# Channel shuffle on one core: giving even and odd tiles each their own DMA queue

## The chip, the cores and the metric

The kernel runs on one core of one Trainium2 chip. A core has five engines that run side by side and are kept in step by semaphores, and a set of 16 DMA engines that move data between device memory and the on-chip buffer of 128 partitions (SBUF). A transfer is started by an instruction that sits in the instruction queue of one of the engines; here SyncE (SP in the profile) and ScalarE (ACT) do that, and neither computes anything. VectorE (DVE) does the only computation. The metric is device time in microseconds of one execution.

## The reference

The input is a float32 array of 16 x 64 x 64 pixels with 256 channels. The channels are seen as 8 groups of 32 and the two axes are swapped, so nothing is calculated: 67.11 MB are read, their order within each pixel is changed, and 67.11 MB are written.

```python
batch, h, w, c = x.shape            # 16, 64, 64, 256
x = x.reshape(batch, h, w, groups, c // groups)     # groups = 8
x = x.transpose(0, 1, 2, 4, 3)
x = x.reshape(batch, h, w, c)
```

## The kernel before

The pixels are cut into 16 tiles. A tile of size q holds 128 x q pixels, q of them in each partition, so every partition's share of a tile is one contiguous run of q x 1024 bytes in memory. The sizes (`_SIZES`) grow at the start and shrink at the end: 4, 8, 16, then twelve times 38, then 28. In bytes: 512 KB, 1 MB, 2 MB, twelve times 4864 KB, 3584 KB.

Each tile t goes through three steps, called here Lt, Ct and St:

- **Lt**, the load into an input buffer (line 47), issued from SyncE's queue.
- **Ct**, one VectorE copy from the input buffer to an output buffer that swaps the two channel axes by its access patterns (line 49).
- **St**, the store of the output buffer (line 53), issued from ScalarE's queue.

There are three input buffers (`_IN_BUFS`) and two output buffers (`_OUT_BUFS`). So L(t+3) may start only when Ct has read its buffer, and C(t+2) may start only when St has landed. The order of the instructions in each queue is the order of the program text (`manual_schedule`), and the waits on semaphores are put in by the framework. SyncE's queue therefore holds L0, L1, L2, ... and ScalarE's holds S0, S1, S2, ...; each engine sends its instructions in that order, and one that waits holds up those behind it. The transfers that a queue has sent form one line of rows on each of the 16 DMA engines; a row is what one partition gets or gives, 38912 bytes for the tiles of size 38. A transfer of 128 rows gives 8 rows to each DMA engine, and a closing packet of a few bytes that reports completion.

Of the kernel before, what the change touches and what calls it, by code (L numbers as in the profile page):

```python
# [1 line left out]

# [4 lines left out]


F32 = mybir.dt.float32
P = 128  # L10

_SIZES = [4, 8, 16] + [38] * 12 + [28]
_IN_BUFS = 3
_OUT_BUFS = 2


@with_exitstack
def kernel(
    ctx: ExitStack,
    tc: tile.TileContext,  # L20
    x: bass.AP,
    groups: bass.AP,
    out: bass.AP,
):
    nc = tc.nc
    b, h, w, c = x.shape
    G = int(groups)
    CPG = c // G
    assert G * CPG == c
    assert sum(_SIZES) * P == b * h * w  # L30
    biggest = max(_SIZES)

    x_flat = x.rearrange("b h w c -> (b h w c)")
    out_flat = out.rearrange("b h w c -> (b h w c)")

    in_pool = ctx.enter_context(tc.tile_pool(name="in_pool", bufs=_IN_BUFS))
    out_pool = ctx.enter_context(tc.tile_pool(name="out_pool", bufs=_OUT_BUFS))

    def rows(flat, first, q):

        return flat[first * c : (first + P * q) * c].rearrange("(p f) -> p f", p=P)

    ctx.enter_context(tc.manual_schedule(engines=None))
    first = 0
    for q in _SIZES:
        in_tile = in_pool.tile([P, biggest * c], F32, name="in_tile")
        nc.sync.dma_start(out=in_tile[:, : q * c], in_=rows(x_flat, first, q))  # L47
        out_tile = out_pool.tile([P, biggest * c], F32, name="out_tile")
        nc.vector.tensor_copy(  # L49
            out=out_tile[:, : q * c].rearrange("p (i j g) -> p i j g", j=CPG, g=G),  # L50
            in_=in_tile[:, : q * c].rearrange("p (i g j) -> p i j g", g=G, j=CPG),
        )
        nc.scalar.dma_start(out=rows(out_flat, first, q), in_=out_tile[:, : q * c])
        first += P * q


# [1 line left out]
_INS = ['x', 'groups']  # L58
_OUTS = [((16, 64, 64, 256), 'float32')]

_NUMBERS = {'groups': 8}


# [26 lines left out]
```

## Time and profile before

| | |
|---|---|
| median of 3 runs | 316.71 us (316.44 to 317.62) |
| the profiled execution's own time | 316.46 us |
| its span (first to last instruction) | 314.7 us |
| VectorE busy | 119.2 us, 16 copies |
| one copy of size 38 | 8802 ns mean |
| DMA traffic | 134.22 MB, mean 427 GB/s over the span |

The profile was taken on one execution. Its span leaves 1.76 us of that execution's own time outside (316.46 less 314.7). "Time to landing" is the time from the start of the issuing instruction to the moment at which all 16 DMA engines have reported completion. q1 is the DMA queue fed by SyncE and q10 the one fed by ScalarE. A view over a short window counts a packet in the window in which it starts.

### The profile page before, as it was taken

Reading aid. Unit: us, or ns where it says so; the run is one execution under the profiler, and the core shown is the slowest. Engines: PE = TensorE matmul, PEld = TensorE weight load, DVE = VectorE, ACT = ScalarE, POOL = GpSimd, SP = SyncE. Lnnn points to the kernel's source line nnn. Section 1 sums busy time; section 2 is a strip of 40 time slices with the busy share of each in tenths; the row PEclk is TensorE's granted clock in tenths of the full one; section 3 lists DMA queues with packets and bytes.
Section 4 is the critical chain, followed back from the end, with each engine's and each line's share of the span. In section 5 each row is a group of like instructions: output and inputs, shape, how many; then the busy total and the mean of one; then the engine's idle time right before and its main releaser. Section 6 shows DMA issues by size and latency. Waiting matters only on the chain.

```text
span 314.7 us, 133 instructions
## 1 busy us (share of the span) xinstructions
DVE 119.2 (38%) x16; POOL 0.2 (0%) x4
## 2 busy tenths in 40 slices
DVE  3040645505506407407308209109109019046620
POOL 0000000000000000000000000000000000000000
DMA  8999999999999999999999999999999999999997
GB/s 308 452 398 454 413 419 466 396 475 396 455 415 445 425 430 440 425 445 415 455 396 470 401 465 406 460 411 460 411 460 411 460 411 455 428 395 454 455 418 306
DMA packets 4608, 134.22 MB, mean 427 GB/s; under 512 B 512, under 2 KB 512, under 8 KB 768
## 3 DMA queue, kind: packets, MB, share of 16 engines
q1 hardware_dynamic: 2304, 67.11, 49.8%
q10 hardware_dynamic: 2304, 67.11, 49.4%
HBM read 67.11 MB, written 67.11 MB: 427 GB/s over the span
## 4 chain that ended last, share of the span: by engine, by line
DMA 75%; DVE 20%; issue 0%; SPq 0%; DVEq 0%
DMA out_dram<-out_tile 74%; DVE out_tile L49 20%; DMA in_tile<-in_x_dram 2%; SPq L47 0%; DVEq L49 0%
## 5 line engine op out<-in xcount | busy, mean ns | idle before, releaser
L49 DVE COPY out_tile<-in_tile 128x9728 f32<-128x9728 f32 (+4 forms) x16 | 119.2, 7449 | 181.4 <-DMA out_dram<-out_tile 175.9
L71 POOL MEMSET const-bfloat16-1.0<- 128x1 bf16 x1 | 0.1, 102 | 0.0
L71 POOL MEMSET const-uint8-127<- 128x1 uint8 x1 | 0.1, 102 | 0.0
L71 POOL MEMSET const-float32-1.0<- 128x1 f32 x1 | 0.1, 99 | 0.0
L71 POOL MEMSET const-float32-0.0<- 128x1 f32 x1 | 0.1, 98 | 0.2 <-issue 0.2
## 6 DMA issues: line engine op xcount, KB each, us to landing
in_tile<-in_x_dram SPq DMA_DIRECT2D x12, 4864.0 KB, 46.8
out_dram<-out_tile ACTq DMA_DIRECT2D x12, 4864.0 KB, 37.0
in_tile<-in_x_dram SPq DMA_DIRECT2D x1, 3584.0 KB, 43.8
out_dram<-out_tile ACTq DMA_DIRECT2D x1, 3584.0 KB, 13.3
in_tile<-in_x_dram SPq DMA_DIRECT2D x1, 2048.0 KB, 11.0
out_dram<-out_tile ACTq DMA_DIRECT2D x1, 2048.0 KB, 26.7
in_tile<-in_x_dram SPq DMA_DIRECT2D x1, 1024.0 KB, 5.4
out_dram<-out_tile ACTq DMA_DIRECT2D x1, 1024.0 KB, 25.8
```

The source lines that it names most:

```text
L49: nc.vector.tensor_copy(out=out_tile[:, : q * c].rearrange("p (i j g) -> p i j g", j=CPG, g=G), in_=in_tile[:, : q * c].rearrange("p (i g ...
L71: nc = _bacc.Bacc("TRN2", target_bir_lowering=False, num_devices=1)
```

## The change

Before, all loads are issued by SyncE and all stores by ScalarE. After, tile t's load and its store are both issued by the same engine: SyncE for even t, ScalarE for odd t. The loads are also written out in another place of the program: the first three stand ahead of the loop, and L(t+3) is issued in iteration t, after St. Sizes, buffers, the copy and all transfers stay as they are.

```diff
-    first = 0
-    for q in _SIZES:
-        in_tile = in_pool.tile([P, biggest * c], F32, name="in_tile")
-        nc.sync.dma_start(out=in_tile[:, : q * c], in_=rows(x_flat, first, q))
+    firsts = [P * sum(_SIZES[:t]) for t in range(len(_SIZES))]
+    in_tiles = {}
+
+    def queue(t):
+
+        return nc.scalar if t % 2 else nc.sync
+
+    def load(t):
+        q = _SIZES[t]
+        in_tiles[t] = in_pool.tile([P, biggest * c], F32, name="in_tile")
+        queue(t).dma_start(
+            out=in_tiles[t][:, : q * c], in_=rows(x_flat, firsts[t], q)
+        )
+
+    for t in range(_IN_BUFS):
+        load(t)
+    for t, q in enumerate(_SIZES):
+        in_tile = in_tiles.pop(t)
         out_tile = out_pool.tile([P, biggest * c], F32, name="out_tile")
         nc.vector.tensor_copy(
...
-        nc.scalar.dma_start(out=rows(out_flat, first, q), in_=out_tile[:, : q * c])
-        first += P * q
+        queue(t).dma_start(
+            out=rows(out_flat, firsts[t], q), in_=out_tile[:, : q * c]
+        )
+        if t + _IN_BUFS < len(_SIZES):
+            load(t + _IN_BUFS)
```

The two queues then hold:

```
SyncE   : L0 L2 S0 L4 S2 L6 S4 L8 ... L14 S12 S14
ScalarE : L1 L3 S1 L5 S3 L7 S5 L9 ... L15 S13 S15
```

## The prediction

> **What bounds the kernel now.** I read the page's slices first. The DMA row stands at 9 in nearly every slice, while the DVE row swings between 0 and 9, so the 16 DMA engines are the resource that is never free.
>
> ```profile
> DVE  3040645505506407407308209109109019046620
> DMA  8999999999999999999999999999999999999997
> ```
>
> Next comes the chain that ended last. It is store, copy, store, copy to the end: each copy waits for the store two tiles back to give its output buffer free. The groups say the same in time: almost all of VectorE's idle time ends with a store.
>
> ```profile
> DMA out_dram<-out_tile 74%; DVE out_tile L49 20%; DMA in_tile<-in_x_dram 2%; SPq L47 0%; DVEq L49 0%
> L49 DVE COPY out_tile<-in_tile 128x9728 f32<-128x9728 f32 (+4 forms) x16 | 119.2, 7449 | 181.4 <-DMA out_dram<-out_tile 175.9
> ```
>
> That chain could be read as "the buffers bound it". The third view corrects this: the DMA view over two steady tile periods, 74 to 120 us, then over the end, 290 to 313 us.
>
> ```profile
> DMA packets 576, 19.92 MB, mean 433 GB/s; under 512 B 64, under 2 KB 64, under 8 KB 64
> q1 hardware_dynamic: 288, 9.96, 50.1%
> q10 hardware_dynamic: 288, 9.96, 50.1%
> ```
>
> ```profile
> DMA packets 325, 9.90 MB, mean 430 GB/s; under 512 B 37, under 2 KB 37, under 8 KB 37
> q10 hardware_dynamic: 325, 9.90, 99.6%
> ```
>
> Two things are to be seen. With both queues at work each gets half of the packets and of the time, and the sum is 433 GB/s; with one queue alone, stores only, it is 430 GB/s. So the rate depends neither on how many queues are filled nor on the mix of reads and writes. And the engines are full: the stores are slow because they share, not because they start late.
>
> A row's price follows. In the timeline the copies of size 38 start 22.97 us apart in the middle (143.32, 166.32, 189.28, 212.26). In such a period a DMA engine moves 8 rows of a load and 8 of a store, so a 38912-byte row takes 22.97 / 16 = 1.436 us. All rows: 16 x 1.436 x (12 + 56/38) = 309.6 us, where 56 is 4 + 8 + 16 + 28. The span is 314.7: some 1.7 us pass before the first row moves, 0.8 lie behind the last landing (the last store is issued at 300.6 and lands after 13.3), and 2.6 are lost in and around the small rows of the start. No order of transfers can gain more than these few; the order can lose, wherever both queues are empty at once.
>
> **What the Trainium skill says.** "DMA: Bandwidth & Descriptors", section "Issuing engines are not separate DMA queues": transfers from sync and scalar run on the same 16 engines and interleave, and issuing from several saves only issue time. The 433 and 430 GB/s above agree. The same page, "Queues, rings and completion order": a DMA engine takes turns between the queues packet by packet, and within a queue takes them in ring order. The 288 against 288 packets agree. "Perfetto Trace Analysis", "DMA Optimizations", advises one engine for inputs and another for outputs, to allow more dynamic spread; that is the arrangement of before, and no trace here prices leaving it.
>
> **The change part by part.** *Issue time.* The tile view has 16 load issues of 328 ns on SP and 16 store issues of 362 ns on ACT. After, each engine issues 8 and 8; nothing else runs on either, so nothing is delayed by more than one issue, 0.36 us, and that lies under rows already in line. Cost 0 in the middle; without the cover, 0.4 us.
>
> *Waits in a queue.* SyncE has L4 (waits for C1), S2 (C2), L6 (C3), S4 (C4); ScalarE has S1 (C1), L5 (C2), S3 (C3). Both are in the order of the copies, so no instruction holds up one that is ready. When Ct ends, St and L(t+3) are both free and stand at the heads of different queues, as before. Cost 0.
>
> *The lines on the DMA engines.* This is the real change. St no longer has a line of stores before it but L(t+2), and L(t+3) stands behind S(t-1). Suppose L(t+2) and S(t-1) began together. They take turns row by row and end together after 16 rows, 22.97 us; then St and L(t+3) begin together. One store always runs against one load, which is the share of before, and a period stays 22.97 us. The next pair is in line in time: C(t+1) starts when S(t-1) lands and takes 8.80 us, about 1 us more brings its pair to the engines (estimate below), and that leaves some 13 us of the running pair. Cost 0; if a pair were late, its whole lateness.
>
> *Do the pairs begin together?* L0 and L1 do, with 8 rows each. Then L2 runs alone until C0 has ended and L3 is in line. L2's rows are 16 KB, 0.61 us. L0 ends near 6 us where it ended at 4.06 (it now shares; harmless, since L1 and L2 fill the engines), C0 takes 1.08, and L3 is in line at about 8. By then four or five of L2's eight rows are out. If the engines switched at once, three or four would be left to share with L3, and L3 would run that many rows ahead of S0 to the end of the kernel. The trace of before speaks against it. S0 was issued at 5.20 us behind no other store, and in the trace's packets its first row moves near 9.5, after five rows of L2. Taking 1 us from issue to the line, the engines were committed about five rows ahead. Then all of L2 is committed when L3 comes, and L3 starts level with S0. I take that.
>
> *The end.* There is no L16, so behind S12 SyncE's line is empty until S14, which waits for C14, which waits for S12. Only S13 is left to cover. From the landing of S12: 0.08 us to the copy, 8.76 (the last size-38 copy), 0.04 to the issue, about 1.0 to the first row: 9.9 us. The 1.0 is an estimate: the first load landed 3.3 us after its issue, its eight 4096-byte rows need 1.3 of these, and I halve the remaining 2. If S12 and L15 end level, S13 still has its 8 rows, 11.5 us. That covers 9.9 by 1.6. The landing comes later than the last row on most engines, by 0.5 us and up to one row where an engine is a turn behind, so the gap is 0 to 0.5: I take **0.4**. Each row of S13 that is already out when S12 ends takes 1.44 us of the cover. After S14 has begun nothing more opens: its 11.5 us cover C15 (6.54 us) and its issue, and S15 follows.
>
> *Sum.* 316.46 (the profiled execution) + 0 + 0 + 0.4 = 316.9; the median shown is 0.25 above that execution, so **317.1** for a median.
>
> *Unknown.* A load behind a store in one line is not in the trace before. Bounds: it could help by at most the 2.6 us lost around the start, and it could cost a row's time at each of 15 changes of pair, 21 us. I take 0, because the engines already change between a read and a write at every row, at 433 GB/s.
>
> **The rivals.** *Slower: the lines are out of step.* If the five rows of commitment do not carry over (they were seen with 16-KB rows, behind one queue), L3 runs three or four rows ahead of S0, each odd store three or four rows ahead of its place, and S13 has only five or four rows left when S12 ends. The gap is 9.9 + 0.5 less 7.2 or 5.7: 3.2 to 4.7 us, at one place, with both queues empty behind S12. That gives 319.9 to 321.4. It decides against me from about two rows: 10.4 less 8.6 is 1.8. For it speaks that the start is fragile, since a delay of 0.6 us there is a whole row; against it, the late first row of S0.
>
> *Slower by mixing.* A change from store to load in one line costs something at each pair; 0.3 us at 15 places would be 4.5, so 321. The equal rates speak against it.
>
> *Faster.* L0 and L1 start from two engines, and the small rows of the start overlap better. In the first 5 us 242 GB/s were moved, 1.21 MB; at 433 GB/s from 1.7 us on it would have been 1.43, so 0.5 us can be had there: 316.2. All 2.6 us would be 314.1, which needs every small loss to go.
>
> *It does not do what it says.* If a hidden wait kept the old order of transfers, both lines would still be filled and the time would stay at 316.7.
>
> **How the numbers follow.** 0.5%, 1.6 us here, is about what a measurement of this kernel can tell from no change. In step, with a gap of 0 to 1.5: 0.58, and nothing changed or a small gain at the start: 0.03; together same 0.61. Out of step, or a gap of over 1.6: 0.29; slower by mixing: 0.07; together slower 0.36. Faster by over 1.6: 0.03. The likeliest case's own range is 316.2 to 318.2. For 8 in 10 the range takes in most of the out-of-step case, to 321.0; it begins at 316.1.
>
> **What would show it right or wrong.** Right: each queue carries 67.11 MB, half loads and half stores; copies of size 38 start 23.0 us apart all along; S12 and L15 land within a row of each other; the DMA row shows no dip, or under 0.5 us, between 290 and 303 us. Out of step: the copies' distances alternate, short and long, with a sum of 46 us, and the DMA rate dips once ahead of S14. Mixing: the period grows beyond 22.97 with the DMA row still at 9. I am wrong altogether if the middle of the kernel, not its end, holds the difference.

## The result: slower by 5%, and the profile after

The kernel after takes 333.5 us in the median of 4 runs, the kernel before 316.97 us: a ratio of 1.051 (95% interval 1.047 to 1.055). One of the four executions, 337.65 us, was in a slower state and does not enter the ratio. The forecast was 317.1 us, with 316.1 to 321.0 as its range. The profiled execution of after took 331.85 us with a span of 330.1 us, 15.4 us more than the span before.

The page after, first the slices. The DVE row is as loose as before, with the engine idle more than half of the time, and the DMA row stands at 9 as before; it dips once shortly before the end.

```profile
DVE  1104092902802803702803602703603604608620
DMA  8999999999999999999999999999999999996996
```

The same page, the packets by DMA queue, and the group of the copies:

```profile
DMA packets 4608, 134.22 MB, mean 407 GB/s; under 512 B 512, under 2 KB 512, under 8 KB 768
## 3 DMA queue, kind: packets, MB, share of 16 engines
q10 hardware_dynamic: 2304, 69.21, 50.4%
q1 hardware_dynamic: 2304, 65.01, 47.1%
...
L63 DVE COPY out_tile<-in_tile 128x9728 f32<-128x9728 f32 (+4 forms) x16 | 119.7, 7484 | 196.4 <-DMA out_dram<-out_tile 189.7
```

This is where the first half of the answer stands. The packets and the bytes are those of before, 4608 and 134.22 MB, and the copies cost the same 119 us. But the shares add up to 97.5% of 330.1 us, 321.8 us of busy time on a mean DMA engine, where before 99.2% of 314.7 us was 312.2. So 9.6 us are **the same packets taking longer**, and the rest, 8.3 us against 2.5, is 5.8 us of DMA engines **with nothing to do**. Together 15.4.

Where? The windows view of after, four stretches of the middle, then one of the end (columns: stretch, its length, DVE busy, POOL busy, clock, DMA share, GB/s):

```profile
66.00:115.00 49.00, 17.63 (x2) 0.00 (x0) 1.00 1.00 416
115.00:164.00 49.00, 17.85 (x2) 0.00 (x0) 1.00 1.00 417
164.00:213.00 49.00, 17.79 (x2) 0.00 (x0) 1.00 1.00 415
213.00:262.00 49.00, 17.75 (x2) 0.00 (x0) 1.00 1.00 414
...
298.00:308.00 10.00, 8.77 (x1) 0.00 (x0) 1.00 0.60 257
```

In the middle the DMA engines are fully busy (1.00) and move 414 to 417 GB/s; before they moved 433. They were full at a lower rate with the same packets, so the packets were slower and no transfer was missing. At the end, ahead of S14, the share falls to 0.60: 10 us at 257 GB/s in place of 433 are 4.1 us lost.

The timeline gives the period, the distance from one copy to the next. These are C5 and C13, first in before (line 49), then in after (line 63):

```profile
74.00 8.80 DVE L49 COPY out_tile<-in_tile 128x9728 f32<-128x9728 f32 x1 [14.22 <-DMA out_dram<-out_tile]
258.23 8.82 DVE L49 COPY out_tile<-in_tile 128x9728 f32<-128x9728 f32 x1 [14.21 <-DMA out_dram<-out_tile]
...
80.75 8.84 DVE L63 COPY out_tile<-in_tile 128x9728 f32<-128x9728 f32 x1 [15.46 <-DMA out_dram<-out_tile]
276.76 8.77 DVE L63 COPY out_tile<-in_tile 128x9728 f32<-128x9728 f32 x1 [15.22 <-DMA out_dram<-out_tile]
```

In after they are 8 periods of 24.50 us apart, in before 8 of 23.03. Eight times 1.47 us are 11.8 of the 15.4 us, so most of the loss lies in the middle of the kernel.

The trace's packets show which rows are long. The records don't name the DMA engine. I fitted each packet to the one that ended just before it, which gives 16 chains, one for each DMA engine; the fit leaves a few packets uncertain. One chain of each kernel follows: L is a row of a load, S a row of a store, a dot a closing packet, and a number stands where a row of 38912 bytes took other than 1.44 us:

```
before   L S . S L S L S L S L . L S L S L S L S . S L S L S L S L . L S
after    L S L S L S L S L S L S1.6 L S1.6 L S . . S2.6 L1.6 S L S L S L S L S L S L S L1.9 .
```

Before, the closings of loads and stores stand four rows of each line apart on most DMA engines. In after, on ten of the 16, a load and a store start together and end together; I call this **in step**: row i of the one goes directly before row i of the other. From 66 to 280 us the 94 rows that come directly after two closings side by side are 0.60 us too long on average, which is 3.5 us for each DMA engine; the other 2141 rows are 0.039 us too long, another 5.3 us. In before no kind of row is over 0.004 us too long on average.

On the other six DMA engines of after the closings mostly fall one row apart. They have fewer long rows and run ahead: 4.2 us are lost in long rows there, on average, against 11.5 us on the ten. So the DMA engines spread. The 16 reports of S12 arrive between 283.8 and 297.8 us, where in before they came within 1.7 us (277.5 to 279.2). A landing counts when the last has reported, so C14 waits for the slowest. The first of them are through with S13 at 299.6 us and then have nothing until the first rows of S14 at 307.6: that is the dip at the end. The kernel keeps the pace of its slowest DMA engines, which have long rows and no gap.

### The profile page after: what moved, and what is told of

Read it like the earlier page. It is cut to its first block, busy times and chain, and to the rows that moved or that the text cites. A ratio compares the mean times of both kernels' runs of the same rounds, so it can differ in the third digit from the quotient of the medians.

```text
span 330.1 us, 134 instructions
## 1 busy us (share of the span) xinstructions
DVE 119.7 (36%) x16; POOL 0.2 (0%) x4
## 2 busy tenths in 40 slices
DMA packets 4608, 134.22 MB, mean 407 GB/s; under 512 B 512, under 2 KB 512, under 8 KB 768
## 4 chain that ended last, share of the span: by engine, by line
DMA 76%; DVE 19%; issue 0%; DVEq 0%
DMA out_dram<-out_tile 74%; DVE out_tile L63 19%; DMA in_tile<-in_x_dram 2%; DVEq L63 0%
```

## The experiments

The pad used below is one small transfer from the input into a buffer that nobody reads. With n = 4 it puts 4 short rows on each DMA engine. With its closing packet these are five more turns for one queue's line, which moves that much later against the other:

```diff
+    pad = pad_pool.tile([P, 128], F32, name="pad")
...
+        if t == 5:
+            nc.scalar.dma_start(
+                out=pad[: 16 * 4, :],
+                in_=x_flat[: 16 * 4 * 128].rearrange("(p f) -> p f", f=128),
+            )
```

**1. New program order, old queues.**

```diff
-        queue(t).dma_start(        # load
+        nc.sync.dma_start(
...
-        queue(t).dma_start(        # store
+        nc.scalar.dma_start(
```

> The program order of after (three loads ahead of the loop, L(t+3) behind St), but all loads on SyncE and all stores on ScalarE as before. Coincident closings (my theory: in after, a load and a store end on a DMA engine together, both closing packets stand side by side, and the next row waits for their completion): the arrangement of the two lines is that of before, closings four rows apart, so 316 to 318 us, copies 22.97 us apart. If the new program order itself were the cause: near 333 us. Mixing (a load behind a store in one line costs): 316 to 318 as well, since no line is mixed.

Measured: 316.67 us, ratio 1.000 (0.999 to 1.001). The new order of the program costs nothing; all of the loss comes from the choice of queues.

**2. After, with the 4-row pad on ScalarE's queue ahead of S5.**

> After, with one small extra transfer on ScalarE's queue ahead of S5: 64 partitions x 512 bytes from the input into a buffer of its own that nobody reads, so 4 short rows on each DMA engine. It moves ScalarE's line four turns later against SyncE's. Coincident closings: from there on the closings are four rows apart, no row is long, the copies' mean distance returns to 23.0 us, the spread between DMA engines at a landing stops growing at about 5 to 7 us, and S13 has 12 rows left when S12 ends, so the idle stretch ahead of S14 goes: 317 to 321 us. Mixing: nothing changes in the lines' contents, so 331 to 335 us. Bad start (the small rows of L0 and L1 in two lines put the DMA engines out of step and the rest follows): the spread is there already, so 330 or more.

Measured: 333.8 us, ratio 1.051 (1.044 to 1.059). My expectation failed. The packets show why this doesn't speak for the rival "mixing" either. SyncE's line ran dry after the pad, and the DMA engines moved three to six rows of ScalarE's queue in a row. On about half of them both lines then began the next pair together again, in step; on the others they stayed one to three rows apart for longer. So the pad neither kept the lines apart nor left them as they were.

**3. The same on SyncE's queue** (`nc.sync` in place of `nc.scalar`).

> The same extra transfer on SyncE's queue, ahead of S5 in program order. Coincident closings: the closings are apart as well and the period returns to 23.0 us, but now S12 is four rows late against S13, so S13 has only four rows left when S12 ends and the idle stretch ahead of S14 is longest, some 5 to 7 us: 320 to 325 us, slower than the pad on ScalarE by 3 to 6 us. Mixing: 331 to 335. Bad start: 330 or more.

Measured: ratio 1.025 (1.019 to 1.030), single executions from 323 to 334 us. The ratio comes from the two shortest, 323.1 and 326.0 us, in which about half of the loss went. The pad's effect was not the same each time; nothing is rested on it.

**4. The kernel before, with the 4-row pad on ScalarE's queue.** No queue is mixed here: one holds loads alone, the other stores and the pad.

> The kernel before (loads on SyncE, stores on ScalarE), with the same 4-row extra transfer on ScalarE's queue ahead of S5. In before the closing of a load and of a store are four rows apart on 13 of 16 DMA engines; the pad shifts the stores by four turns, so they coincide. Coincident closings: from about 110 us on the first row after each pair of closings takes 2.0 to 2.9 us, 0.6 to 1.4 us lost in each of 8 tile periods: 321 to 328 us, with the copies 23.6 to 24.5 us apart. Mixing or bad start: no line is mixed and the start is that of before, so 316 to 318 us.

Measured: 325.3 us, ratio 1.027 (1.025 to 1.029). This is the turning point: one transfer of 32 KB costs 8.7 us in a kernel whose queues are as before. The DMA view of it over four periods, 150 to 247 us:

```profile
DMA packets 1160, 40.16 MB, mean 414 GB/s; under 512 B 128, under 2 KB 128, under 8 KB 128
## 3 DMA queue, kind: packets, MB, share of 16 engines
q10 hardware_dynamic: 580, 20.08, 52.5%
q1 hardware_dynamic: 580, 20.08, 47.9%
```

Equal packets and bytes, but the stores (q10) need 52.5% of the time and the loads (q1) 47.9%; before, it was 50.1% each. The rate is 414 GB/s, as in after. One chain:

```
pad 4    . . L S1.6 L S1.6 L S1.6 L S1.6 L S1.6 L S1.6 L S1.6 L S1.6 . . L S1.6
```

My first theory, that closings side by side make the next row wait, is refuted by this run. The row after the two closings is not long here (0.000 us over the 70 of them between 126 and 280 us). The long rows are the store rows that come directly after the load row of the same number: from 150 to 247 us they are 0.16 us too long on average. Eight such rows are 1.3 us a period; the copies between 126.19 and 270.51 us are 24.05 us apart, 1.1 us more than before. The two DMA engines whose closings fall one row apart have almost no long rows.

Being in step is not enough by itself, however. In the first pair in step, from 105 to 126 us, only 55 of 110 such store rows are long, the later ones of the pair.

**5. The kernel before, with 5 rows in the pad.**

> As the 4-row pad on the kernel before, with 5 rows on each DMA engine instead of 4. Same row in step (my new theory: where a DMA engine moves row i of a load and directly after it row i of a store, the store's row takes 1.6 us instead of 1.44): now store row i follows load row i+1, so no row is long, and the time is 316 to 318 us. Coincident closings: the closing packets stand one row apart instead of side by side; if nearness is what costs, 320 to 326 us. The pad itself (its own transfer and semaphore): 325 us as with 4 rows.

Measured: 317.9 us, ratio 1.004 (1.003 to 1.005). One turn more, and all but 1.2 us are gone: a store row then follows load row i+1, and the closings stand one row apart. So the 8.7 us are not the pad's own cost, and they don't come from closings that are merely near. They need loads and stores that are **in step to the row**.

**6. The kernel before with the 4-row pad, results of tiles 3 to 14 stored 3.67 MB further on.** The last tile's result takes the place that becomes free, so the tiles of the output stand in another order.

```diff
+    place = firsts[:3] + [f + last for f in firsts[3:-1]] + [firsts[3]]
-        nc.scalar.dma_start(out=rows(out_flat, first, q), ...)
+        nc.scalar.dma_start(out=rows(out_flat, place[t], q), ...)
```

> The kernel before with the 4-row pad, and the results of tiles 3 to 14 stored 3.67 MB further on (the last tile's result is put ahead of tile 3's, so the output's tiles are in another order). Rows stay in step as with the pad alone: the same partitions of SBUF, closings side by side; only the distance in device memory between the row read and the row written changes, by 94.3 rows. Same row in step through device memory: the distance no longer clashes, 316 to 319 us. Same row in step through SBUF or inside the DMA engine: 324 to 326 us as before the move. Coincident closings: 324 to 326.

Measured: 325.1 us, ratio 1.027 (1.023 to 1.031). With this other distance in device memory the cost stays whole. It is one other distance, not every one.

**7. After, with the same move.**

> After, with the results of tiles 3 to 14 stored 3.67 MB further on, as in the run above (output's tiles in another order). Device memory: the long rows go, what stays is the idle stretch at the end and the long first rows, 318 to 326 us. SBUF or the DMA engine: 331 to 335 us, unchanged. Mixing: 331 to 335.

Measured: 334.0 us, ratio 1.055 (1.052 to 1.058). Unchanged too.

**8. After, with a 2-row pad on ScalarE's queue ahead of S1** (`t == 1`, n = 2).

> After, with a pad of 2 short rows on each DMA engine on ScalarE's queue ahead of S1, so at the start and before the DMA engines have drifted apart; ScalarE's line then runs three turns behind SyncE's. Same row in step: rows are never in step, spread at a landing stays under 5 us, the copies' mean distance is 23.0 us, S13 has 10 or 11 rows left when S12 ends: 316.5 to 320 us. Mixing: 331 to 335. If the lines lock together again by themselves, as they did after the pad of 4 rows: 328 to 334 us, with the in-step pattern back in the packets after a few tiles.

Measured: 337.0 us, ratio 1.065 (1.062 to 1.068), the third of the three cases. The DMA view of it from 52 to 64 us shows the lines locking again:

```profile
## 3 DMA queue, kind: packets, MB, share of 16 engines
q10 hardware_dynamic: 94, 3.04, 58.8%
q1 hardware_dynamic: 48, 1.87, 41.3%
```

ScalarE's line (q10) moves twice the packets of SyncE's (q1), which has run dry: its next transfers, L6 and S4, wait for the copies C3 and C4, and L6 is issued only at 53.1 us. L6 and S3 then start level. That it happens here, and not with the later pad of run 9, I put down to the short tiles of the start; this is argued, not tested. From 64 us on the closings are side by side.

**9. After, with the 2-row pad on ScalarE's queue ahead of S5** (`t == 5`, n = 2), past the short tiles.

> After, with the pad of 2 short rows (three turns with its closing) on ScalarE's queue ahead of S5, so after the short tiles of the start, where neither line runs empty. S5 and what follows on ScalarE's queue should then run three turns behind SyncE's. In step (a load and a store that start together on a DMA engine lose time, in whichever line they stand): from about 105 us on the rows are two to four turns apart, nearly no row is long, the copies' mean distance is 23.0 to 23.3 us, and S13 has about 11 rows left when S12 ends, so the idle stretch ahead of S14 goes: 318 to 323 us. Mixing (a load behind a store in one line): 330 or more, since every line is as mixed as in after. Lines lock again by themselves: 328 to 336.

Measured: 321.9 us, ratio 1.014 (1.011 to 1.018). From 110 us on there are no two closings side by side, and the rows are 0.003 us too long on average, with every line as mixed as in after. Two thirds of the loss are gone by one transfer of 16 KB. Of the 5 us that remain, some 2.4 us are a gap of the DMA engines near the end.

**10. The same pad on SyncE's queue ahead of S4.**

> The same pad of 2 rows on SyncE's queue ahead of S4: SyncE's line runs three turns behind ScalarE's. In step: nearly no long rows from about 105 us on, but S13 is three rows further when S12 ends, so 4 to 6 us are idle ahead of S14: 321 to 328 us, 3 to 6 us more than with the pad on ScalarE's queue. Mixing: 330 or more, both pads alike.

Measured: two executions of 319.2 and 319.4 us against 316.9 for before; two others took 331.9 and 335.7 us and have no trace, so whether they fell into step is open. In the traced one the copies C6 and C12 are 137.8 us apart, 22.97 a period, and the rows of the middle are less than 0.001 us too long on average. The end went as expected in kind, though with less than 4 to 6 us. S14 is issued at 295.4 us here, and the gap ahead of it lies between 290 and 296 us (columns of the windows view as above):

```profile
290.00:296.00 6.00, 6.00 (x2) 0.00 (x0) 1.00 0.56 240
```

In the packets the gap is 2.1 us on the mean DMA engine, which is nearly all that this execution takes more than before.

**11. The kernel before with loads and stores cut in halves of 64 partitions, in opposite orders.**

```diff
+        for h in (0, 1):
+            nc.sync.dma_start(out=in_tile[64 * h : 64 * h + 64, : q * c], ...)
...
+        for h in (1, 0):
+            nc.scalar.dma_start(out=rows(...)[64 * h : 64 * h + 64, :], ...)
```

> The kernel before with each load cut in two transfers, partitions 0 to 63 and then 64 to 127, and each store cut in two in the other order, 64 to 127 first: 4 rows on each DMA engine per transfer, twice as many closings, loads on SyncE and stores on ScalarE. It is to show where loads and stores stand against each other with halves, and whether store rows are long when a load row of other partitions goes before them. Same partition: wherever a lower half of a load runs beside an upper half of a store, no row is long; where like halves run side by side in step, store rows take 1.6 us. In step alone: store rows are long in both cases. Time by the first 316 to 320 us or 320 to 326, according to how they fall; by the second 322 to 328 if they fall in step.

Measured: 455.4 us in the median of two; the traced one moved a mean of 293 GB/s. A miss: from 110 to 400 us a load row takes 2.44 us on average and a store row 1.58, so the halves slow the rows by more than what was to be seen, and nothing about partitions in step can be read from it.

**12. The kernel before with the 4-row pad, output buffers moved up by 8320 bytes inside their partitions.**

```diff
+    pad = pad_pool.tile([P, 2080], F32, name="pad")
     out_pool = ctx.enter_context(tc.tile_pool(name="out_pool", bufs=_OUT_BUFS))
```

> The kernel before with the 4-row pad, and the output buffers moved up by 8320 bytes within their partitions (the pad's buffer, made that large, now lies between the input and the output buffers). Rows in step as with the pad alone. Place within SBUF: if the row written and the row read clash by their addresses inside a partition, another distance takes the clash away, 316 to 319 us. Same partition whatever the address, or something inside the DMA engine: 324 to 326 us as without the gap.

Measured: 322.7 us, ratio 1.017 (1.015 to 1.020), between the two expectations. In the packets the long store rows take 1.5 to 1.6 us as without the gap, but they come later: in the first pair in step (105 to 126 us) 1 of 104 such rows is long, where it was 55 of 110 without the gap. So this distance inside the partition delays and lessens the clash and doesn't remove it.

**13. After, but the queues are mixed only from tile 3 on.**

```diff
+    def load_queue(t):
+        return nc.sync if t < 3 else queue(t)
+    def store_queue(t):
+        return nc.scalar if t < 3 else queue(t)
```

> After, but tiles 0 to 2 are loaded by SyncE and stored by ScalarE as before; only from tile 3 on does each parity have its own queue. Start decides (the short first tiles let both lines begin a pair together, and from then on they stay in step): here SyncE's line runs empty near 35 to 42 us while ScalarE's goes on, L6 joins in the middle of L5, and the pairs are some four rows apart: 317 to 323 us, few long rows, spread at a landing under 4 us. If the two lines fall into step by themselves whatever the start: 328 to 336 us, closings side by side.

Measured: **316.8 us, ratio 1.000 (0.999 to 1.002)**. Thirteen of sixteen tiles have their load and store on one queue as in after, and the whole loss is gone. Its DMA view from 120 to 213 us:

```profile
DMA packets 1162, 40.12 MB, mean 431 GB/s; under 512 B 131, under 2 KB 131, under 8 KB 131
## 3 DMA queue, kind: packets, MB, share of 16 engines
q1 hardware_dynamic: 583, 20.08, 49.9%
q10 hardware_dynamic: 579, 20.04, 49.8%
```

and its timeline of four copies:

```profile
175.02 8.76 DVE L71 COPY out_tile<-in_tile 128x9728 f32<-128x9728 f32 x1 [21.59 <-DMA out_dram<-out_tile]
190.66 8.79 DVE L71 COPY out_tile<-in_tile 128x9728 f32<-128x9728 f32 x1 [6.88 <-DMA out_dram<-out_tile]
220.98 8.77 DVE L71 COPY out_tile<-in_tile 128x9728 f32<-128x9728 f32 x1 [21.54 <-DMA out_dram<-out_tile]
236.61 8.72 DVE L71 COPY out_tile<-in_tile 128x9728 f32<-128x9728 f32 x1 [6.85 <-DMA out_dram<-out_tile]
```

The distances alternate, 15.64 and 30.32 us, with 45.96 for two tiles: the sign that the prediction named for lines out of step. Here it goes with no loss at all. In after the distances are nearly even, 25.41 and 24.04 us:

```profile
178.46 8.80 DVE L63 COPY out_tile<-in_tile 128x9728 f32<-128x9728 f32 x1 [14.60 <-DMA out_dram<-out_tile]
203.87 8.99 DVE L63 COPY out_tile<-in_tile 128x9728 f32<-128x9728 f32 x1 [16.62 <-DMA out_dram<-out_tile]
227.91 8.89 DVE L63 COPY out_tile<-in_tile 128x9728 f32<-128x9728 f32 x1 [15.04 <-DMA out_dram<-out_tile]
```

## Why the prediction was wrong

**The bound** was read rightly: the DMA engines are full, 9 in nearly every slice before and after, and VectorE's 119 us are no limit.

**Issue time and waits in a queue**: costed at 0, and nothing in the runs speaks against it. With the queues mixed from tile 3 on, the same waits and the same issues take 316.8 us.

**The lines on the DMA engines** is the step that failed. Its picture was right on most DMA engines: L0 and L1 begin together, L3 starts level with S0 (near 11.4 us), and from then on St and L(t+3) begin and end together, as the landings show (S7 at 178.34 us, L10 at 178.16). Its price was wrong. "One store always runs against one load, which is the share of before, and a period stays 22.97 us": the share is that of before, but the period is 24.50 us. I took the cost of a row, 1.436 us, as fixed, because it had been the same for stores alone and for loads with stores. But rows in step can take 1.6 us and more: from 66 to 280 us the long rows cost 8.8 us on the mean DMA engine. In the steady part of before no row i of a store stood behind row i of a load: its lines were four or five rows apart. The price of the step was not in the trace before, and I put no bound on it; the bound I gave, "a row's time at each of 15 changes of pair", was laid to mixing. The prediction's own sign of being wrong altogether came true: the middle, not the end, holds most of the difference.

**The end**: 0.4 us were forecast for the gap ahead of S14, about 4 were lost. The working (9.9 us to cover, 8 rows of S13 to cover them) took all 16 DMA engines as one, with a turn between them at most. By the landing of S12 they were 14 us apart, because some had many long rows and some few. Those ahead had about one row of S13 left, where eight were counted on.

**The rivals.** "The lines are out of step", my slower case, has the sign wrong. Out of step is what before is, and what the late pads of 2 rows and the mixing from tile 3 bring about, at about 23 us a period. I had priced only its end, where S13 would be ahead. A gap of that kind is seen in run 10, 2.1 us; with mixing from tile 3 there is none, and 445 GB/s are moved from 284 to 298 us, around the issue of S14 at 289. "Slower by mixing" named the sign that came, a longer period with the DMA row at 9, but falls as a mechanism of its own: mixed lines without step cost nothing (run 13), and step without mixed lines costs 8.7 us (run 4). One part of the loss is seen only with both: after two closings the first row takes 2.04 us on average in after, and up to 2.9, but 1.44 with the pad on before. So mixing adds to the cost of being in step.

**What the forecast leaned on.** The Trainium skill, "DMA: Bandwidth & Descriptors", section "Issuing engines are not separate DMA queues", holds that transfers issued from several engines run on the same 16 DMA engines and interleave, and that issuing from several at once only saves issue time. The first half agrees with the chains. Against the "only" stands the measurement, which decides: the same transfers in the same program order take 317 us (run 1) or 333 us (after), by their queues alone.

**What stays open** is why a store row takes 1.6 us when the load row of the same number goes before it, and why it does not always. With the pad on before, 650 of 716 such store rows from 126 to 280 us are long, but only half in the first pair. In after, from 66 to 280 us, 140 of 304 are, and so are 63 of 271 load rows behind the store row of the same number. So long rows come in number only in the runs in which most DMA engines are in step (in after some fall on the others too), but something else, which no run isolates, has to come with it. Another distance in device memory and another distance inside the partition didn't remove it. The two rows lie in the same partition of SBUF if row numbers go with partitions, and in whole transfers of 128 partitions equal row numbers always mean equal partitions, so the two could not be parted; the halves of run 11, meant to part them, were too slow to show it. How the DMA engines stand against each other was not varied either. Why two of four executions of run 10 took 332 us and more is open as well.

## What to carry to other kernels

A full DMA row is not the end of the reading: compare the rate in GB/s in a steady stretch, 433 before and 415 after here. Where the queues carry equal bytes, unequal shares tell which queue has the long packets, as in run 4. When transfers of the same shape share the DMA engines, their order against each other can matter: look how far apart loads and stores run, and test a change of queues with one small extra transfer that shifts a line by a few rows. And where a landing needs all DMA engines, look at the spread of their reports; here it grew without a sign in the slices and part of it was paid at the end.

## What the hardware showed that was not expected

- With the 4-row pad on before, most store rows of 38912 bytes that directly follow the load row of the same number on their DMA engine take 1.6 us instead of 1.44 (650 of 716). One turn further on they take 1.44 (run 5). The long rows don't all come at once: the first pair in step had them in half of the places.
- The phase of two queues against each other lasts: in run 4 a shift of five turns at 110 us was still there at 270 us. It was lost in runs 2 and 8 where one of the lines ran dry; in run 8 both then began together, in run 2 on about half of the DMA engines.
- DMA engines don't wait for each other: in after the reports of one transfer spread from 3.0 us (77.7 to 80.7) to 14.0 us (283.8 to 297.8).
- With transfers cut in halves of 64 partitions the kernel moved a mean of 293 GB/s, where with those of 128 it moved 427.
